# Conv2d 3x3 with 2x2 max pooling: merged row differences, one PSUM bank per image, 22 four-product steps and a new order of all operations

## The chip, the core and the metric

The kernel runs on one core of one Trainium2 chip. The metric is the device time in microseconds of one execution; lower is better. Names of engines in the profile: PE multiplies matrices (PEld loads their weights), DVE, ACT and POOL work element by element, SP issues most of the DMAs (queues of DMA issues are written SPq, ACTq, POOLq).

## The reference

Sixteen images with 64 channels of 64x64 are convolved with a 3x3 kernel (padding 1) to 128 channels, and the result is pooled by the maximum over 2x2.

```python
batch, c_in, h, w, c_out, k = 16, 64, 64, 64, 128, 3
x_pad = np.pad(x, ((0, 0), (0, 0), (pad, pad), (pad, pad)), mode='constant')
for kh in range(k):
    for kw in range(k):
        conv[b, co] += weight[co, ci, kh, kw] * x_pad[b, ci, kh:kh+h, kw:kw+w]
output[b, c, i, j] = np.max(conv[b, c, i*2:(i+1)*2, j*2:(j+1)*2])
```

## The kernel before

**The arithmetic.** Two conv rows that are pooled together, 2i and 2i+1, need four input rows: x(-1), x0, x1, x2. With g0, g1, g2 the three rows of the 3x3 weights, each of them three taps over columns, there are two ways to make them.

- A *five-product step* (K): the sum A = (g2-g1) x1 + g0 x(-1), the sum B = (g0-g1) x0 + g2 x2, and the common part R = g1 (x0 + x1). The pooled rows are max(A, B) + R. The products are called PA (two of them), PB (two) and PR. Only one row sum, KS = x0 + x1, has to be made.
- A *four-product step* (W): with E = x1 - x0, Z = x(-1) - x1, Y = x2 - x0 and S = x0 + x1, and GM = (g0+g2-g1)/2, GP = (g0+g1+g2)/2, the sum A is P2 = GM E plus P0 = g0 Z, the sum B is P2 with the other sign plus P3 = g2 Y, and P1 = GP S is common. Here four sums of rows (KS has one) are made on DVE or POOL, but PE has one product less.

Each product is three column taps (kw) for each of the two images of a pair. Channels are 64, so the two images of a pair lie on the two halves of the 128 rows of the array, and the two matmuls of a tap run at the same time, 512 columns each (8 output rows of 64).

**The steps.** A step is a quarter (8 pooled rows of 32) of a pair of images. There are 8 pairs x 4 quarters = 32 steps: 16 of K on the even pairs and 16 of W on the odd ones, one of each per turn of the loop. That makes 16 x 5 + 16 x 4 = 144 products of six matmuls, 864 matmuls.

**The way of a step.** PE writes A into one of four accumulators `acc` [128, 2, 8, 64], which hold two banks each, one for either image. For W, once P2 is there, ACT writes minus A into another accumulator as the start of B (`seed`, L301) while P0 is added to A. ACT copies A to SBUF (`evac`, L292, tile `ev`); DVE takes the maximum of B and `ev` in place (`rowmax`, L305); PE adds the common product PR or P1; ACT copies the odd columns (`odd`, L310, tile `od`); DVE takes the maximum of even columns and `od` (`colmax`, L324, tile `o`), and SP (in the end once ACT) stores it. All these work on 1024 elements per row (both images) or 512 after pooling of the rows; only in the last step on one image at a time. An accumulator is handed on through the list `free` when its last reader has been issued.

**Row operations.** `row_op` (L250) makes the sums of rows, 512 elements each: KS and WS on DVE, WZ and WY on POOL, WE on DVE up to step 4 and on POOL after that. `on_vector` and `on_gpsimd` tie each POOL operation behind the last one that DVE has done on SBUF. The W pairs lie in SBUF as fp32 in two buffers `wx`, the K pairs as bf16 in `kx`, cast by the DMA (POOL's queue, L95), except the first quarters, which come as fp32 and are cast by DVE (L340) and ACT (L347).

**Loads.** `wload(i + 4)` is issued behind the store of K's step i; `kload` brings half a pair of images at a time, one pair ahead, behind WY of quarters 1 and 2. So W quarters come four turns, K halves about three turns ahead.

**The order.** The scheduler is off; every engine works through its instructions in the order in which the program issues them. `HEAD`, `STEADY` (turns 4 to 12) and `TAIL` are lists written by hand. At the start the weights are loaded, combined (D2 = g2-g1, D0 = g0-g1, GM, GP), turned by PE (`turn`, L151) and copied out (`turn_out`, L163 to L169); eight matmuls on ones run ahead of that (L403).

Of the kernel before, what the change touches and what calls it, by code (L numbers as in the profile page):

```python
# [8 lines left out]


@with_exitstack
def kernel(
# [7 lines left out]

    nc = tc.nc
# [10 lines left out]
    NP = B // 2  # L45
    NQ = 4
    R = HO // NQ
    N = NP * NQ // 2
    assert N == 16
# [3 lines left out]
    row_pool = ctx.enter_context(tc.tile_pool(name="row_pool", bufs=2))  # L53
    ev_pool = ctx.enter_context(tc.tile_pool(name="ev_pool", bufs=3))
    od_pool = ctx.enter_context(tc.tile_pool(name="od_pool", bufs=3))
    o_pool = ctx.enter_context(tc.tile_pool(name="o_pool", bufs=4))
# [4 lines left out]
    acc = [psum.tile([128, 2, R, W], FP32, name=f"acc_{i}") for i in range(4)]  # L61
    free = deque(range(4))
    unset = set(range(4))

    SYNC = mybir.DependencyInfo(mybir.DependencyClass.Sync, mybir.DependencyReason.DATA)
    sbuf_op = [None]
# [5 lines left out]
    def on_vector(inst):  # L74
        sbuf_op[0] = inst
        return inst

    def on_gpsimd(inst):
        behind(inst, sbuf_op[0])
        return inst  # L80

# [4 lines left out]
    def chunk(q):  # L86
        return (2 * R * q + (q > 0), min(H, 2 * R * (q + 1) + 1))

    kx = {}
    wx = [const.tile([128, H + 2, W], FP32, name=f"wx_{i}") for i in range(2)]  # L90

    def kload(j, lo, hi):
        if j not in kx:
            kx[j] = kx_pool.tile([128, H, W], BF16, name="kx")
        return nc.gpsimd.dma_start(out=kx[j][:, lo:hi, :], in_=rows_of(2 * j, lo, hi))  # L95

    def wload(i):
        j, q = divmod(i, NQ)
        lo, hi = chunk(q)
        return nc.sync.dma_start(  # L100
            out=wx[j % 2][:, lo + 1 : hi + 1, :], in_=rows_of(2 * j + 1, lo, hi)
        )

    wraw = const.tile([CO, CI * K * K], FP32)
    nc.sync.dma_start(out=wraw, in_=weight.rearrange("a b c d -> a (b c d)"))  # L105
    _, khi = chunk(0)
    kfirst = const.tile([128, khi, W], FP32)
    nc.sync.dma_start(out=kfirst, in_=rows_of(0, 0, khi))
    klo2, khi2 = chunk(1)
    ksecond = const.tile([128, khi2 - klo2, W], FP32)  # L110
# [4 lines left out]
    for t in wx:  # L115
        nc.gpsimd.memset(t[:, 0, :], 0.0)
        nc.gpsimd.memset(t[:, H + 1, :], 0.0)

    D2, G0, D0, G2, GM, G1, GP = range(1, 29, 4)
    BLOCKS = {"D2": D2, "G0": G0, "D0": D0, "G2": G2, "GM": GM, "G1": G1, "GP": GP}
    wq = const.tile([CO, 29, CI], BF16)
    wt = const.tile([128, 28, CO], BF16)
    gsum = const.tile([CO, 3, CI], FP32)
# [5 lines left out]
    def slots(m):  # L131
        return wq[:, m : m + 3, :]

    def zero(t, h):
        return nc.tensor.matmul(
            acc[t][:, h], zeros[:, 0:128], zeros, start=True, stop=True, skip_group_check=True
        )

    turned = {}

    def turned_cols(m):
        lo, hi = BLOCKS[m] - 1, BLOCKS[m] + 3
        tp = acc[turned[m]][:, int(m == "G1")].rearrange("p a b -> p (a b)").bitcast(BF16)
        return lo, hi, tp[:, 0 : (hi - lo) * 128]

    def turn(m):
        turned[m] = turned["GM"] if m == "G1" else free.popleft()
        unset.add(turned[m])
        lo, hi, tp = turned_cols(m)
# [7 lines left out]
    def turn_out(m):  # L157
        if m != "GM":
            free.append(turned[m])
        lo, hi, src = turned_cols(m)  # L160
        dst = wt[:, lo:hi, :].rearrange("p a b -> p (a b)")
        if m == "GM":
            nc.scalar.mul(dst, src, 0.5)  # L163
        elif m == "GP":
            nc.vector.tensor_scalar_mul(out=dst, in0=src, scalar1=0.5)
        elif m in ("G0", "G2"):
            nc.scalar.copy(out=dst, in_=src)
        else:
            nc.vector.tensor_copy(out=dst, in_=src)  # L169


    def taps(t, m0, rows, start=False, skip=None, only=None):
        dst = acc[t]
        if start:
            unset.discard(t)
        for kw in (1, 0, 2):
            i0, i1 = 0, R
            if skip == 0:
                i0 = 1
            if skip == R - 1:  # L180
                i1 = R - 1
            o0, o1, c0, c1 = (0, W, 0, W) if kw == 1 else (1, W, 0, W - 1) if kw == 0 else (0, W - 1, 1, W)
            for half in range(2) if only is None else (only,):
                lo = half * CI
                nc.tensor.matmul(  # L185
                    dst[:, half, i0:i1, o0:o1],
                    wt[lo : lo + CI, m0 + kw - half, :],
                    rows(lo, i0, i1, c0, c1),
                    start=start and kw == 1,
                    stop=True,  # L190
                    skip_group_check=True,
                )

    def step1(t, q):
        first = q * R
        return lambda lo, i0, i1, c0, c1: t[lo : lo + CI, first + i0 : first + i1, c0:c1]

    def step2(t, first):
        return lambda lo, i0, i1, c0, c1: t[
            lo : lo + CI, first + 2 * i0 : first + 2 * (i1 - 1) + 1 : 2, c0:c1  # L200
        ]

    ta, tb = {}, {}

    def pa(i):
        j, q = divmod(i, NQ)
        t = ta["k", i] = free.popleft()
        taps(t, D2, step2(kx[j], 2 * q * R + 1), start=True)
        taps(t, G0, step2(kx[j], 2 * q * R - 1), skip=0 if q == 0 else None)

    def pb(i):
        j, q = divmod(i, NQ)
        t = tb["k", i] = free.popleft()
        taps(t, D0, step2(kx[j], 2 * q * R), start=True)
        taps(t, G2, step2(kx[j], 2 * q * R + 2), skip=R - 1 if q == NQ - 1 else None)

    def pr(i):
        taps(tb["k", i], G1, step1(row["ks", i // NQ], i % NQ))

    def p2(i):  # L220
        t = ta["w", i] = free.popleft()
        taps(t, GM, step1(row["we", i // NQ], i % NQ), start=True)

    def p0(i):
        taps(ta["w", i], G0, step1(row["wz", i // NQ], i % NQ))

    def p3(i):
        taps(tb["w", i], G2, step1(row["wy", i // NQ], i % NQ))

    def p1(i, h=None):  # L230
        taps(tb["w", i], GP, step1(row["ws", i // NQ], i % NQ), only=h)
# [4 lines left out]
    def row_out(name, i):  # L236
        j, q = divmod(i, NQ)
        if (name, j) not in row:
            row[name, j] = row_pool.tile([128, HO, W], BF16, name=name)
        return row[name, j][:, q * R : (q + 1) * R, :]  # L240
# [214 lines left out]
```

## Time and profile before

| | us |
|---|---|
| median of 3 runs (lowest, highest) | 108.33 (107.81, 108.77) |
| span of the profiled execution, first to last instruction | 106.18 |
| difference of median and span | 2.15 |
| first matmul of a product | 5.96 |
| last column maximum ends | 103.03 |

The profiled execution is one execution; its time is known by its span alone. The page shows each engine's busy time and share of the span; the "chain" goes back from the last instruction through what released each step. In a line of a group stand the source line, engine, operation, tiles, shapes and count, then the busy time and the mean in ns, then idle time ahead of them with what ended it. In a line of the timeline stand start and duration in us, engine, line, operation, tiles, shapes and the number of instructions merged. In a line of DMA issues the last two numbers are the size and the median time from issue to landing.

### The profile page before, as it was taken

The numbers are of one execution on the slowest core, as the hardware profiler recorded it, in microseconds if no ns is written. First come the engines' busy times: TensorE is split into PE (matmuls) and PEld (weight loads), VectorE is DVE, ScalarE is ACT, GpSimd is POOL, SyncE is SP. The second block draws the span as 40 slices with busy tenths as digits, with TensorE's granted clock in tenths as the row PEclk, the third lists the DMA queues.
The fourth block names the chain that finished last, engine by engine and source line by source line (L and its number), as shares of the span: only waits on it lengthen the run. The fifth ranks groups of instructions, "written<-read, shape, count | busy, mean of one in ns | idle before, by whom it ended". The sixth has DMA issues, their size and how long they took to land.

```text
span 106.2 us, 2337 instructions
## 1 busy us (share of the span) xinstructions
PE 98.7 (93%) x900; PEld 51.2 (48%) x900; DVE 82.3 (78%) x115; ACT 72.3 (68%) x92; POOL 60.6 (57%) x70
## 2 busy tenths in 40 slices
PE   7879999999999999999999999999999999999800
PEld 2444445555555555555555555555555555455300
DVE  1598989889797868696977868687879688668940
ACT  4628976776867677777677676767877776775620
POOL 6208691915439494949385694949293947653000
PEclk9999999999999999999999999999999999999975
DMA  2987999999968589999968399999966503232071
GB/s 53 370 269 269 228 152 314 264 304 304 316 245 211 190 177 187 219 298 195 337 253 208 124 210 202 265 257 213 385 188 167 195 4 122 78 107 96 0 247 49
DMA packets 12619, 21.96 MB, mean 207 GB/s; under 512 B 960, under 2 KB 9280, under 8 KB 12608
## 3 DMA queue, kind: packets, MB, share of 16 engines
q1 hardware_dynamic: 11312, 18.03, 52.9%
q0 software_dynamic: 1152, 3.65, 20.1%
q8 instruction: 7, 0.11, 0.4%
q10 hardware_dynamic: 144, 0.13, 0.4%
q14 instruction: 4, 0.03, 0.2%
HBM read 17.07 MB, written 8.39 MB: 240 GB/s over the span
## 4 chain that ended last, share of the span: by engine, by line
PE 84%; DVE 6%; DMA 4%; ACT 1%; issue 1%; SPq 0%; ACTq 0%; DVEq 0%
PE acc L185 83%; DVE acc L305 5%; DMA kfirst<-in_x_dram 4%; PE acc L151 1%; DVE o L324 1%; ACT od L310 1%; DVE kx L340 0%; SPq L105 0%; ACTq L333 0%; DVEq L305 0%
## 5 line engine op out<-in xcount | busy, mean ns | idle before, releaser
L185 PEld LDWEIGHTS <-wt 64*128 64x128 bf16 x864 | 48.6, 94 | 45.1 <-issue 1.8
L305 DVE TENSOR_TENSOR acc<-acc,ev 128x1024 f32<-128x1024 f32 (+1 forms) x34 | 39.5, 1166 | 11.9 <-PE acc L185 11.4
L185 PE MATMUL acc<-kx,wt 64*128 64x504 bf16 (+3 forms) x384 | 46.6, 373 | 0.6 <-DVE kx L340 0.6
L292 ACT COPY ev<-acc 128x1024 f32<-128x1024 f32 (+1 forms) x34 | 32.6, 964 | 12.5 <-PE acc L185 11.0
L250 POOL TENSOR_TENSOR wz<-wx 128x512 bf16<-128x512 f32 x16 | 20.3, 1271 | 30.3 <-DVE ws L250 24.3
L310 ACT COPY od<-acc 128x512 f32<-128x512 f32 (+1 forms) x33 | 19.0, 574 | 12.5 <-PE acc L185 11.5
L324 DVE TENSOR_TENSOR o<-acc,od 128x512 f32<-128x512 f32 (+1 forms) x33 | 22.1, 674 | 4.5 <-ACT od L310 4.4
L250 POOL TENSOR_TENSOR wy<-wx 128x512 bf16<-128x512 f32 x16 | 20.3, 1270 | 0.0
L301 ACT ACTIVATE acc<-acc 128x1024 f32<-128x1024 f32 x16 | 16.1, 1008 | 1.0 <-PE acc L185 0.5
L250 POOL TENSOR_TENSOR we<-wx 128x512 bf16<-128x512 f32 x11 | 14.1, 1278 | 0.1
L185 PE MATMUL acc<-ws,wt 64*128 64x504 bf16 (+1 forms) x96 | 13.3, 377 | 0.4 <-DVE acc L305 0.4
L185 PE MATMUL acc<-ks,wt 64*128 64x504 bf16 (+1 forms) x96 | 13.3, 377 | 0.1
L185 PE MATMUL acc<-we,wt 64*128 64x504 bf16 (+1 forms) x96 | 13.3, 377 | 0.0
L185 PE MATMUL acc<-wz,wt 64*128 64x504 bf16 (+1 forms) x96 | 13.2, 377 | 0.0
L185 PE MATMUL acc<-wy,wt 64*128 64x504 bf16 (+1 forms) x96 | 13.2, 377 | 0.0
L250 DVE TENSOR_TENSOR ws<-wx 128x512 bf16<-128x512 f32 x16 | 10.9, 684 | 0.0
L250 DVE TENSOR_TENSOR ks<-kx 128x512 bf16<-128x512 bf16 x16 | 6.7, 417 | 0.0
L95 POOL DMA_DIRECT2D kx<-in_x_dram x8 | 4.7, 589 | 2.6 <-DVE ks L250 2.6
L403 PE MATMUL acc<-const-bfloat16-1.0 128*128 128x512 bf16 x8 | 3.2, 572 | 0.8 <-PEq L436 0.8
L250 DVE TENSOR_TENSOR we<-wx 128x512 bf16<-128x512 f32 x5 | 3.6, 722 | 0.1
L354 DVE TENSOR_TENSOR wq<-wraw 128x192 bf16<-128x192 f32 x1 | 0.5, 500 | 2.6 <-DMA wraw<-in_weight_dram 2.6
L151 PE MATMUL acc<-ident,wq 128*128 128x128 bf16 x28 | 2.1, 220 | 0.4 <-DVE wq L354 0.4
(26 smaller groups left out, 15.9 us busy)
## 6 DMA issues: line engine op xcount, KB each, us to landing
out_dram<-o SPq DMA_DIRECT2D x31, 256.0 KB, 3.8
wx<-in_x_dram SPq DMA_DIRECT2D x8, 512.0 KB, 6.8
wx<-in_x_dram SPq DMA_DIRECT2D x4, 544.0 KB, 6.0
wx<-in_x_dram SPq DMA_DIRECT2D x4, 480.0 KB, 4.8
kx<-in_x_dram POOLq DMA_DIRECT2D x3, 528.0 KB, 8.3
kx<-in_x_dram POOLq DMA_DIRECT2D x3, 496.0 KB, 8.7
kfirst<-in_x_dram SPq DMA_DIRECT2D x1, 544.0 KB, 4.3
ksecond<-in_x_dram SPq DMA_DIRECT2D x1, 512.0 KB, 4.9
```

The costliest lines, as they stand in the source:

```text
L95: return nc.gpsimd.dma_start(out=kx[j][:, lo:hi, :], in_=rows_of(2 * j, lo, hi))
L151: nc.tensor.transpose(tp[:, (j - lo) * 128 : (j - lo + 1) * 128], wq[:, j : j + 2, :].rearrange("a b c -> a (b c)"), ident,)
L185: nc.tensor.matmul(dst[:, half, i0:i1, o0:o1], wt[lo : lo + CI, m0 + kw - half, :], rows(lo, i0, i1, c0, c1), start=start and kw == 1, sto ...
L250: return engine.tensor_tensor(out=row_out(name, i), in0=row_in(t, f + a, pad), in1=row_in(t, f + b, pad), op=op)
L292: nc.scalar.copy(out=ev[g][:, halves(h)], in_=acc[ta[g]][:, halves(h)])
L301: nc.scalar.mul(acc[t], acc[ta["w", i]], -1.0)
L305: nc.vector.tensor_tensor(out=t, in0=t, in1=ev[g][:, halves(h)], op=MAX)
L310: nc.scalar.copy(out=od[g][:, halves(h)], in_=acc[tb[g]][:, halves(h), :, 1::2])
L324: nc.vector.tensor_tensor(out=o, in0=acc[tb[g]][:, s, :, 0::2], in1=od[g][:, s], op=MAX)
L354: on_vector(nc.vector.tensor_sub(out=slots(D2), in0=g2, in1=g1))
L403: warm = nc.tensor.matmul(acc[n // 2][:, n % 2], ones[:, 0:128], ones, start=True, stop=True, skip_group_check=True)
```

## The change

Almost every line of the kernel is written anew; the arithmetic of a step stays. What differs:

1. **10 K steps and 22 W steps** instead of 16 and 16. `SEQ` gives their sequence. K has pairs 0 and 1 and half of pair 2, W the rest. That is 10 x 5 + 22 x 4 = 138 products.
2. **One difference over 16 rows, V** (`rv`), takes the place of Z and Y: input rows shifted by two, subtracted for all 16 rows at once, 1024 elements. Its even rows are minus Z, its odd rows Y; P0 and P3 read every second row of it. E changes its sign too, so A has the other sign, `evac` of W multiplies by -1 and `seed` copies as it is.
3. **One bank for each image.** `acc` is eight tiles of one bank. `EV`, `SE`, `MX`, `OD`, `CM` exist for each image by itself: 64 each (44 of SE), of 512 elements, or 256 after pooling of the rows. Products are issued for each image too; two that stand next to each other in the order, on different images, are interleaved tap by tap, and they may be different products. Four products have no partner. The first K step's products are halved (4 rows each) to begin on half of the load.
4. **Loads** of a quarter at a time for both kinds: 24 quarters as fp32 on SP (step 0's in two pieces, K step 3 cast by ACT), 8 casting loads on POOL's queue. From step 7 on, the load of step s waits for both column maxima of step s-7 (`paced`, `AHEAD`). There are four `wx` buffers; the row sums have a pool of 8 small tiles, V one of 6, `ev` and `od` 8, `o` 12.
5. **Engines and order.** `ORDER`, one list of tokens, gives the order of all instructions, the engine of each row operation (v, a, g for DVE, ACT, POOL) and the bank of each sum. DVE has 10 KS, 14 E, 8 S and 9 V, POOL 8 E, 14 S and 13 V. A POOL row operation is still tied behind the last one of DVE in the list (`row_op`).

```diff
+SEQ = "KWWKWWKWWKWWKWWWKWWKWWKWWKWWKWWW"
+ORDER = """
+LW c.g0:a c.GS:v c.D0:v c.GM:v T.G0:0 c.g2:a LX.1 c.g1:a T.D0:1 LX.0a T.GM:2 c.D2:v E.1:v TV.G0:a
...
+CM.6.0 PBa.9.0:5 P0.7.1 OD.6.1 EV.7.1 MX.9.1 MX.8.0 LK.12 P2.7.0:2 P3.7.1 ST.3 CM.6.1 PBb.9.0
+P2.8.1:6 MX.7.1 S.10:g SE.7.0:1 S.7:g SE.8.1:0 E.10:v P1.8.0 PR.9.1 MX.9.0 OD.9.1 CM.9.1 OD.8.0
+S.11:g P1.7.1 P0.7.0 OD.7.1 EV.7.0 E.11:g P3.7.0 P0.8.1 CM.7.1 MX.7.0 PR.9.0 P3.8.1 PAa.12.1:4
...
+ST.23 S.30:g ST.26 EV.30.0 OD.29.0 MX.30.1 EV.31.1 P1.31.0 P3.31.1 MX.30.0 P1.30.1 P1.30.0 CM.29.0
+OD.31.0 MX.31.1 CM.31.0 OD.30.1 ST.25 CM.30.1 ST.29 ST.31.0 P1.31.1 OD.30.0 CM.30.0 OD.31.1 ST.30.1
+ST.30.0 CM.31.1 ST.31.1
+"""
...
-    acc = [psum.tile([128, 2, R, W], FP32, name=f"acc_{i}") for i in range(4)]
-    free = deque(range(4))
+    acc = [psum.tile([128, R, W], FP32, name=f"acc_{i}") for i in range(8)]
...
+    last_row = [None]
+    def row_op(e, out, in0, in1, op):
+        inst = eng[e].tensor_tensor(out=out, in0=in0, in1=in1, op=op)
+        if e == "g":
+            behind(inst, last_row[0])
+        else:
+            last_row[0] = inst
...
+    AHEAD = 7
+    def paced(s, inst):
+        for l in (0, 1):
+            behind(inst, done.get((s - AHEAD, l)))
...
+    def load_cast(s):
+        p, lo, hi = chunk(s)
+        paced(s, nc.gpsimd.dma_start(out=kx_of(p)[:, lo:hi, :], in_=rows_of(p, lo, hi)))
...
-    def wz(i):
-        on_gpsimd(row_op(nc.gpsimd, "wz", i, -1, 1, SUB))
-    def wy(i):
-        on_gpsimd(row_op(nc.gpsimd, "wy", i, 2, 0, SUB))
...
+    def rv(s, e):
+        p, q = place[s]
+        t = row["V", s] = v_pool.tile([128, 2 * R, W], BF16, name="wv")
+        f = 2 * R * q
+        u = wx[p % NWX]
+        row_op(e, t, u[:, f + 2 : f + 2 + 2 * R, :], u[:, f : f + 2 * R, :], SUB)
...
+        "P0": ("A", pw("G0", "V", False, 2, 0)),
+        "P3": ("B", pw("G2", "V", False, 2, 1)),
...
+    def evac(s, l):
+        t = ev[s, l] = ev_pool.tile([128, R, W], FP32, name="ev")
+        if SEQ[s] == "W":
+            nc.scalar.mul(t, acc[bank["A", s, l]], -1.0)
+        else:
+            nc.scalar.copy(out=t, in_=acc[bank["A", s, l]])
...
+    def flush():
+        for group in zip(*unit):
+            for tap in group:
+                tap()
+        unit.clear()
```

In a token such as `P0.7.1` stand the product (or operation), the step and the image; `SE.7.0:1` writes bank 1, `S.10:g` runs on POOL, `LX` loads as fp32, `LK` loads and casts, `ST` stores.

More of the change, by code (lines that the diff above doesn't have):

```diff
@@ L1 @@
-from collections import deque
 from contextlib import ExitStack
@@ L89 @@
-    kx = {}
[L90 to L102, printed above, removed]
@@ L104, with chunk @@
-    wraw = const.tile([CO, CI * K * K], FP32)
[L105 to L110, printed above, removed]
+    def chunk(s):
+        p, q = place[s]
+        same = any(place[t] == (p, q - 1) and SEQ[t] == SEQ[s] for t in range(N))
+        lo = 2 * R * q + 1 if same else max(0, 2 * R * q - 1)
+        return p, lo, min(H, 2 * R * (q + 1) + 1)
@@ L175, in taps @@
+    def taps(name, s, l, part):
+        side, of = PRODUCTS[name]
+        block, i0, i1, rows, first = of(s, l, part)
+        t = bank[side, s, l]
+        if first:
             unset.discard(t)
         for kw in (1, 0, 2):
[L177 to L181, printed above, removed]
-            o0, o1, c0, c1 = (0, W, 0, W) if kw == 1 else (1, W, 0, W - 1) if kw == 0 else (0, W - 1, 1, W)
[L183 to L192, printed above, removed]
@@ L211, in pb @@
[L211 to L225, printed above, removed]
@@ L406 @@
-        if n == 3:
-            behind(wload(0), warm)
-    kx[0] = kx_pool.tile([128, H, W], BF16, name="kx")
-    def run(order):
-        for s in order.split():
-            name, *args = s.split(".")
-            steps[name](*map(int, args))
-    run(HEAD)
-    for i in range(FIRST, LAST + 1):
-        for s in STEADY.split():
-            steps[s[:-2]](i + int(s[-2:]))
-    run(TAIL)
+        nc.tensor.matmul(
+            acc[n], ones[:, 0:128], ones, start=True, stop=True, skip_group_check=True
+        )
```

457 lines of the change are left out of this document (253 added, 204 removed).

## The prediction

> **What bounds the kernel now.** I read the page first (busy shares, chain by engine), then the chain of waits in order of time, the groups by form, and the timeline at both ends. From the page and the chain in order of time:
>
> ```profile
> PE 98.7 (93%) x900; PEld 51.2 (48%) x900; DVE 82.3 (78%) x115; ACT 72.3 (68%) x92; POOL 60.6 (57%) x70
> PE 84%; DVE 6%; DMA 4%; ACT 1%; issue 1%; SPq 0%; ACTq 0%; DVEq 0%
> ...
> 5.96 1.39 PE acc L185 x12
> ...
> 9.64 81.42 PE acc L185 x756
> ...
> 102.61 0.42 DVE o L324
> ```
>
> PE sets the time: 756 matmuls follow one another in 81.42 us, 0.1077 us each (two run at once, one on each half of the rows). 864 x 0.1077 = 93.05 us. With 0.9 us of transposes after the first product, PE could go from 5.96 to 99.9; its last six matmuls end at 100.9, so it loses about 1.0 us in all. Behind it come two pairs of odd-column copy and column maximum (to 103.03) and the last store (3.15 us, to 106.18). The profiled span is 106.18 and the median of the runs 108.33, so I add 2.15 us to a span.
>
> The prices come from groups by form (mean ns) and from the distance between neighbours on the timeline of DVE and ACT:
>
> ```profile
> L305 DVE TENSOR_TENSOR acc<-acc,ev 128x1024 f32<-128x1024 f32 x30 | 36.8, 1228 | 11.7 <-PE acc L185 11.4 <-ACT ev L292 0.2
> L305 DVE TENSOR_TENSOR acc<-acc,ev 128x512 f32<-128x512 f32 x4 | 2.7, 696 | 0.2
> L324 DVE TENSOR_TENSOR o<-acc,od 128x256 f32<-128x256 f32 x2 | 0.8, 424 | 1.0 <-ACT od L310 0.8
> L250 POOL TENSOR_TENSOR wy<-wx 128x512 bf16<-128x512 f32 x16 | 20.3, 1270 | 0.0
> L357 POOL TENSOR_TENSOR gsum<-wraw 128x192 f32<-128x192 f32 x1 | 0.8, 824 | 2.4 <-DVE wq L356 2.4
> ```
> ```profile
> 44.79 1.23 DVE L305 TENSOR_TENSOR acc<-acc,ev 128x1024 f32<-128x1024 f32 x1 [0.85 <-PE acc L185]
> 46.00 0.69 DVE L324 TENSOR_TENSOR o<-acc,od 128x512 f32<-128x512 f32 x1
> 46.60 0.42 DVE L250 TENSOR_TENSOR ks<-kx 128x512 bf16<-128x512 bf16 x1
> 46.94 0.69 DVE L250 TENSOR_TENSOR ws<-wx 128x512 bf16<-128x512 f32 x1
> ```
>
> Back to back, DVE starts the next instruction about 0.08 us before the last one ends: 0.60 us for 512 elements, 0.34 for one of 0.42 us, 1.21 for 1024 from acc. By that rule the 696 ns row costs 0.61 and the 424 ns row 0.34.
>
> **The change, part by part.**
>
> *Matmuls.* 10 five-product and 22 four-product steps make 138 products of six, 828 full matmuls (24 extra come from halving early products, two halves for one): 828 x 0.1077 = 89.2 us, 3.9 less.
>
> *Order of the two row halves.* Before, they alternate throughout. Now four products stand alone in the queue (three matmuls on one half) and in some 66 places the order flips. Strictly in order, each single would leave the other half idle (six pair times of 0.215, 1.3 us) and each flip cost the 20 ns between two partners (1.3 us). The last products before show it: they are issued as three on one half and then three on the other, yet take what six alternating ones take.
>
> ```profile
> 98.20 0.83 PE L185 MATMUL acc<-ws,wt 64*128 64x512 bf16 x6
> ...
> 100.07 0.83 PE L185 MATMUL acc<-ws,wt 64*128 64x512 bf16 x6 [0.39 <-DVE acc L305]
> ```
>
> So I cost the order at 0, between 0 and 2.6. The Trainium skill ("TensorE: Matmul & The Clock Gate", Part 3) says that matmuls start and end strictly in program order; by that rule the sum would be 2.6 us longer, and the row above disagrees.
>
> *Start and end of PE.* The first product now needs a four-product chunk of 1152 columns instead of 1088 as second load of the queue. The old one landed at 5.46; 33 KB more at its rate (557 KB from 3.68 to 5.46) is 0.1, and its difference on DVE 0.7: start at 6.3. Eight transposes (0.6) and one zeroing matmul (0.2) follow it. PE's end is 6.3 + 0.8 + 89.2 = 96.3. Behind it one copy (0.38), one maximum (0.43) and the store (3.15), no longer two of each in turn, since each image has its own bank: 100.3. That is the span if PE never waits.
>
> *DVE.* 64 row maxima x 0.61 = 39.0; 64 column maxima x 0.34 = 21.8; nine merged differences of 1024 elements, 1.14 each by the 1024 row = 10.3; 14 E x 0.60 = 8.4; 8 S x 0.60 = 4.8; 10 KS x 0.34 = 3.4; weights, turn-outs and casts of the head 3.4. Sum 91.1, where before gives 80.4 in the same way: halving the instructions doubles their fixed part. From 3.7 (weights landed) DVE could end at 94.8; with the store 97.95. It may lose 2.35 us before it, not PE, sets the end. This is the tightest new number.
>
> *ACT.* 108 copies of 512 at 0.48 (two followed each other by that at 94.61), 64 of 256 at 0.27, 6 us of head: 75. 20 us are free; hidden, if not late.
>
> *POOL.* 22 operations of 512 at 1.23 are 27.1. A merged difference of 1024 isn't in the trace: at least 1.23, at most 2 x 1.23; the 192 and 512 rows give 1.4 ns per element, so 1.95. 13 of them 25.4, casting loads 4.7: 57. Before, the two separate differences cost 2.46 together. Hidden.
>
> *DVE against POOL.* One DVE row operation began before under a running POOL operation:
>
> ```profile
> 10.38 1.26 POOL L250 TENSOR_TENSOR wy<-wx 128x512 bf16<-128x512 f32 x1
> ...
> 11.31 0.88 DVE L250 TENSOR_TENSOR we<-wx 128x512 bf16<-128x512 f32 x1
> ```
>
> It took 0.88 instead of 0.69: 0.20 longer, when 0.33 of the POOL operation was left. Maxima over acc don't suffer (1.23 under POOL and without). The kept order ties each POOL operation behind DVE's last row operation, but not DVE's next behind POOL. Before, KS and WS come together once a step and POOL is done by then. Now 41 row operations are spread among 35 of POOL. I set both on a clock of 0.323 us per product and image along the written order: 15 of the 41 meet a running POOL operation, with 12.3 us left of these in sum; less 0.13 each, 10.3. The written order isn't time, and some stand just behind POOL's end, so the bounds are 0 and 10.3; I take the middle, 5.2. The Trainium skill ("SBUF — State Buffer", Who interferes with whom) says that a VectorE instruction with two SBUF inputs and a GpSimd instruction reading SBUF exclude one another for a whole instruction; the 0.88 row agrees, and by that rule the price goes to the upper end.
>
> *Loads.* A load of step s now waits for the column maxima of step s-7, and the stores ahead of it on SP wait too; a casting load also stands behind POOL's differences. On the same clock, step 12's is issued at about 30.4 (behind V.8) and wanted by PE at 35.0: 4.6 us. Steps 25, 28, 22, 9 have 5.5, 6.1, 6.5, 6.7. From the issues:
>
> ```profile
> kx<-in_x_dram POOLq DMA_DIRECT2D x1, 256.0 KB, 7.5
> kx<-in_x_dram POOLq DMA_DIRECT2D x1, 240.0 KB, 7.9
> ```
>
> Same size, but in the busiest stretch (DMA 0.90 from 10 to 40 us, 0.64 from 70 to 90). Fp32 loads of some 512 KB took 4.3 us (kfirst) to 6.8 (the usual wx), so an estimate for a quiet casting load is 7.5 x 4.3/6.8 = 4.7. At 4.7 the lack is 0.1, at 7.5 it is 2.9 + 2.0 + 1.4 + 1.0 + 0.8 = 8.1; at 6.0, which I take, 1.9. Two thirds of that lies under DVE's lateness, which postpones PE's want: 0.7.
>
> *Sum.* 97.95 + 0.4 (DVE waiting for loads in the head) + 5.2 + 0.7 = 104.25; with 2.15, **106.4**, 1.8% less.
>
> **Rivals.**
> 1. *Nothing is late* (neither port nor loads beyond 0.7): PE bounds, 100.3 + 0.7 + 2.15 = 103.2. For it: PE lost only 1.0 before. Against: DVE would need 97% of its time.
> 2. *DVE bounds, slower.* All 15 meetings cost in full: 97.95 + 0.4 + 10.3 + 0.4 = 109.05, 111.2. Place: KS, E and S on DVE behind V on POOL (V.8, V.18, V.26, V.29). It decides from 8 us of stops. For it: the 0.88 row; against: the order often puts DVE's operation right behind POOL's end.
> 3. *Casting loads late.* 7.5 us each: 100.3 + 8.1 = 108.4, 110.6. For it: every such load before took 7.5 or more; against: half the size of most, and spread out.
> 4. *Strict program order on PE*: 106.4 + 2.6 = 109.0, no change. Against: the six matmuls above.
>
> **How the numbers follow.** 1% (about what a measurement of this kernel can tell) is 107.25 to 109.4. Rival 1 and what lies near it 0.19; my forecast (104.7 to 107.25) 0.36; within 1%: forecast with more port time 0.12, rival 4 0.06; rival 2 0.17; rival 3 0.10. Faster 0.55, same 0.18, slower 0.27. The range is from rival 1 to rival 2, 103.2 to 111.2; the likeliest case alone 104.7 to 107.25.
>
> **What would show it.** PE: 889 instructions, products still 0.1077 each where dense, singles without a gap. DVE busy near 90 us and over 85% of the span. Row operations on DVE (we, ws, wv, ks) longer than 0.69, 0.69, 1.22, 0.42 where POOL runs: their excess is the port's price. PE's idle time put down to kx loads at steps 12 and 25 tells rival 3; to DVE's maxima, rival 2. A merged difference on POOL near 2.0 us. After the last matmul 4.0 us to the end. Wrong would be: DVE with much idle time while PE waits, or ACT as releaser.

## The result, and the profile after

The changed kernel takes 112.69 us (median of 4 runs, 112.57 to 112.99), the kernel before 108.53 on the same chip: ratio 1.040, 95% interval 1.036 to 1.044. It is 4% slower. The forecast was 106.4, 1.8% faster, and its range ended at 111.2. The profiled execution took 112.76 us with a span of 110.99, so 1.77 us lie outside the span. Of some kernels below, single executions lie over 1.5% above the fastest one (137.11 against 132.14 us in 4); the ranges include them, the ratios leave them out.

First the page of the changed kernel: busy time and share of the span by engine, then the chain by engine.

```profile
PE 100.8 (91%) x889; PEld 53.6 (48%) x889; DVE 95.5 (86%) x179; ACT 85.4 (77%) x185; POOL 64.6 (58%) x65
...
PE 26%; DVE 14%; DMA 12%; POOL 7%; ACT 6%; issue 3%; SPq 1%; DVEq 0%; ACTq 0%
```

Before, PE made up 84% of the chain and DMA 4%. Now PE has 26% and DMA 12%, and the rest hops between the engines. No engine is the bound; something hands its lateness round. The chain in order of time (start, duration, what) shows what:

```profile
44.88 5.64 DMA wx<-in_x_dram
...
79.53 7.88 DMA kx<-in_x_dram
...
87.46 12.12 PE acc L340 x108
...
106.08 0.82 PE acc L340 x3
...
106.92 0.38 ACT od L374
...
107.32 0.42 DVE o L379
```

The end is reached through two loads: an fp32 load of SP issued at 44.88 us and a casting load issued at 79.53 that took 7.88 us. TensorE's last matmuls end at 106.90 (96.3 in the forecast, if TensorE never waits), and behind them come one copy, one maximum and the store, 4.1 us (forecast 4.0).

Why the loads are late stands in the waits (who waited for whom: us in total, times, longest). The first line is of SP's queue, where L245 issues the fp32 loads:

```profile
SPq L245 <- DVE o L379: 63.4, 15, 16.1
```
```profile
DVE we L181 <- DMA wx<-in_x_dram: 4.8, 6, 1.9
...
POOL we L181 <- DMA wx<-in_x_dram: 2.9, 1, 2.9
...
PE acc L340 <- DMA kx<-in_x_dram: 1.8, 2, 0.9
```

SP stood 63 us before loads, every time for a column maximum (L379): that is the pacing. In turn DVE, POOL and TensorE waited for the data. The largest single stop, at 29 us on the timeline:

```profile
28.16 1.24 PE L340 MATMUL acc<-kx,wt 64*128 64x504 bf16 x8
28.35 0.69 DVE L181 TENSOR_TENSOR we<-wx 128x512 bf16<-128x512 f32 x1 [1.93 <-DMA wx<-in_x_dram]
...
30.09 0.42 DVE L379 TENSOR_TENSOR o<-acc,od 128x256 f32<-128x256 f32 x1
30.25 2.36 POOL L181 TENSOR_TENSOR wv<-wx 128x1024 bf16<-128x1024 f32 x1 [1.77 <-DVE wv L181]
30.43 0.69 DVE L370 TENSOR_TENSOR acc<-acc,ev 128x512 f32<-128x512 f32 x1
30.56 0.37 PE L340 MATMUL acc<-we,wt 64*128 64x512 bf16 x1 [1.17 <-DVE o L379]
```

The load of step 8 was issued at 21.34 us and landed at 28.25. Its own maxima, those of step 1, had ended at 19.34; but on SP it stands behind the load of step 7, which waited for the maxima of step 0 until 20.94, so the pacing of one load holds the next one too. E.8 and V.7 stand in DVE's order ahead of the column maximum CM.5.0 (the line at 30.09), which frees the bank that the next product of step 8 writes. So E.8's wait held DVE for 1.93 us, POOL stood idle for 1.77 us before V.8, and TensorE stopped 1.33 us longer than a pair of matmuls takes. The bracket at PE names the maximum; the cause stands two instructions ahead of it on DVE.

A simple measure serves for all kernels below: TensorE's *lateness* is how far its products lag behind one full matmul every 0.1077 us, counted from the start of its first product. (At a span of 110.99: first product at 6.35 + 89.2 of matmuls + lateness + 4.11 behind the last.) It is 11.3 us here at the end of the last matmul; in the kernel before it was 1.9. Of the 11.3, the head (to 10.5 us) has 2.5 us; E.8 1.3; E.15, whose load is the one at 44.88, 0.5; the casting loads of steps 25 and 28 1.08 and 1.09; two stops for row operations of POOL at 60 and 62 us 0.22 and 0.38; the last products 0.9; the rest is many small pieces.

The rows that answer to the prediction's prices (mean ns):

```profile
L370 DVE TENSOR_TENSOR acc<-acc,ev 128x512 f32<-128x512 f32 x64 | 42.8, 691 | 2.1 <-ACT ev L355 1.4 <-PE acc L340 0.3 <-ACT ev L357 0.2
...
L181 DVE TENSOR_TENSOR wv<-wx 128x1024 bf16<-128x1024 f32 x9 | 11.6, 1299 | 0.0
...
L181 DVE TENSOR_TENSOR ws<-wx 128x512 bf16<-128x512 f32 x8 | 6.3, 788 | 0.0
L181 DVE TENSOR_TENSOR ks<-kx 128x512 bf16<-128x512 bf16 x10 | 5.2, 517 | 0.0
```
```profile
L181 POOL TENSOR_TENSOR wv<-wx 128x1024 bf16<-128x1024 f32 x13 | 30.7, 2358 | 12.4 <-DVE we L181 4.5
```

Row maxima cost what they should. KS is 517 instead of 417 ns and S 788 instead of 684: these met POOL. A merged difference on POOL costs 2.36 us, not 1.95.

### The profile page after: what moved, and what is told of

It is laid out like the page before. It is cut to its first block, busy times and chain, and to the rows that moved or that the text cites. A ratio compares the mean times of both kernels' runs of the same rounds, so it can differ in the third digit from the quotient of the medians.

```text
span 111.0 us, 2491 instructions
## 1 busy us (share of the span) xinstructions
PE 100.8 (91%) x889; PEld 53.6 (48%) x889; DVE 95.5 (86%) x179; ACT 85.4 (77%) x185; POOL 64.6 (58%) x65
## 3 DMA queue, kind: packets, MB, share of 16 engines
q1 hardware_dynamic: 12480, 21.34, 60.3%
## 4 chain that ended last, share of the span: by engine, by line
PE 26%; DVE 14%; DMA 12%; POOL 7%; ACT 6%; issue 3%; SPq 1%; DVEq 0%; ACTq 0%
PE acc L340 26%; DMA kx<-in_x_dram 7%; DMA wx<-in_x_dram 5%; DVE acc L370 5%; DVE wv L181 4%; DVE o L379 4%; ACT ev L355 4%; POOL ws L181 3%; POOL wv L181 2%; ACT od L374 1%; ACT acc L366 1%; POOL we L181 1%; DVE we L181 1%; SPq L388 1%; DVE ws L181 1%
## 5 line engine op out<-in xcount | busy, mean ns | idle before, releaser
L340 PE MATMUL acc<-wv,wt 64*128 64x504 bf16 (+1 forms) x264 | 55.4, 377 | 0.3 <-POOL wv L181 0.2
L340 PE MATMUL acc<-kx,wt 64*128 64x504 bf16 (+5 forms) x264 | 48.6, 355 | 2.9 <-DMA kx<-in_x_dram 1.8
L370 DVE TENSOR_TENSOR acc<-acc,ev 128x512 f32<-128x512 f32 x64 | 42.8, 691 | 2.1 <-ACT ev L355 1.4
L181 POOL TENSOR_TENSOR wv<-wx 128x1024 bf16<-128x1024 f32 x13 | 30.7, 2358 | 12.4 <-DVE we L181 4.5
L340 PE MATMUL acc<-we,wt 64*128 64x512 bf16 (+1 forms) x132 | 32.3, 377 | 1.7 <-DVE o L379 1.2
L340 PE MATMUL acc<-ws,wt 64*128 64x512 bf16 (+1 forms) x132 | 33.4, 377 | 0.2
L355 ACT ACTIVATE ev<-acc 128x512 f32<-128x512 f32 x44 | 26.1, 602 | 5.2 <-PE acc L340 4.6
L366 ACT COPY acc<-acc 128x512 f32<-128x512 f32 x44 | 25.4, 579 | 5.1 <-DVE o L379 2.8
L374 ACT COPY od<-acc 128x256 f32<-128x256 f32 x64 | 23.1, 377 | 5.5 <-PE acc L340 5.0
L379 DVE TENSOR_TENSOR o<-acc,od 128x256 f32<-128x256 f32 x64 | 24.9, 415 | 1.6 <-ACT od L374 1.3
```

What stands on the lines that cost most here:

```text
L181: inst = eng[e].tensor_tensor(out=out, in0=in0, in1=in1, op=op)
L340: yield lambda kw=kw, o0=o0, o1=o1, c0=c0, c1=c1: nc.tensor.matmul(acc[t][:, i0:i1, o0:o1], wt[l * CI : l * CI + CI, BLOCKS[block] + kw - ...
L355: nc.scalar.mul(t, acc[bank["A", s, l]], -1.0)
L366: nc.scalar.copy(out=acc[b], in_=acc[bank["A", s, l]])
L370: nc.vector.tensor_tensor(out=t, in0=t, in1=ev[s, l], op=MAX)
L374: nc.scalar.copy(out=t, in_=acc[bank["B", s, l]][:, :, 1::2])
```

## The experiments

Three theories. **L, late loads:** the pacing, and places behind other instructions on SP's and POOL's queues, make loads late, and waiting engines pass it on. **P, port:** row operations of DVE stop while POOL works, and the merged difference makes POOL's stretches longer. **D, DVE full:** the halved instructions fill DVE, and loads only show it. Each kernel was timed beside the kernel before.

### 1. The pacing taken away

```diff
-    AHEAD = 7
+    AHEAD = 99
```

> The changed kernel without the tie of a load to the column maxima of seven steps before; the order stays, so on SP a load still stands behind the stores written ahead of it. Theory L (late loads cost most: 1.33 + 0.48 + 1.08 + 1.09 us of PE gaps after the head are ended by a load or by a difference that waited for one): the gaps at E.8 and the casting loads shrink, 1.5 to 4 us faster, 108.7 to 111.2. Theory P (the port that DVE and POOL share, and POOL's 2.36 us for a merged difference, set the pace): loads are only what comes last, within 1 us of 112.7. Theory D (DVE, with 91 us of work in doubled instructions, is full): within 1 us of 112.7 as well.

Measured: 111.05 us (110.53 to 111.36), ratio 1.025 (1.021 to 1.028). The stop at E.8 is gone, the lateness falls from 11.3 to 8.3 us. Two stops stay, 1.42 us for the casting load of step 25 and 0.79 for that of step 28: they stand behind differences on POOL and were issued at 70.29 and 77.05, landing 7.4 and 7.8 us later. L holds for 1.6 us, and shows that the pacing is only part of it.

### 2. All loads from step 7 on earlier, with a pacing of twelve steps

```diff
-    AHEAD = 7
+    AHEAD = 12
```

In `ORDER` each load of a step s from 7 on stands directly behind both CM of step s-12 (if there is none, behind the first loads); among themselves they keep their order.

> The changed kernel with every load from step 7 on moved ahead in the order, behind the column maxima of twelve steps before instead of seven, on both queues. Theory L: no load is late after the head, the four gaps (4.0 us) go and what stood behind them: 107.5 to 109. Theory P: 111.5 to 113, and the excess of DVE's row operations under POOL stays near 2.7 us. Theory D: 111 to 113, DVE's idle time turns into other idle time.

Measured: 113.83 us (113.35 to 115.13), ratio 1.049 (1.045 to 1.054): slower than the changed kernel, the opposite of what L expected. The timeline tells why:

```profile
55.91 0.57 POOL L254 DMA_DIRECT2D kx<-in_x_dram  x1 [2.69 <-DVE o L379]
56.50 2.35 POOL L181 TENSOR_TENSOR wv<-wx 128x1024 bf16<-128x1024 f32 x1
56.90 4.26 DVE L181 TENSOR_TENSOR wv<-wx 128x1024 bf16<-128x1024 f32 x1
58.80 1.26 POOL L181 TENSOR_TENSOR we<-wx 128x512 bf16<-128x512 f32 x1
```

A casting load sits on POOL's queue and waits there for a column maximum, so POOL stood for 2.69 us; V.15 behind it came late and met V.17 of DVE, which took 4.26 us instead of 1.22, through two operations of POOL. TensorE stopped 2.0 us for V.15, and at 31 us 2.4 us for V.8, late in the same way. The experiment had moved a wait onto a busy engine; it does not speak against L, and it shows what P can do.

### 3. POOL's merged differences left out

```diff
+        if e == "g":
+            behind(nc.gpsimd.memset(t, 0.0), last_row[0])
+            return
         row_op(e, t, u[:, f + 2 : f + 2 + 2 * R, :], u[:, f : f + 2 * R, :], SUB)
```

> The changed kernel with the 13 merged differences of POOL replaced by a fill with zeros of the same tile (their products come out as zero): it reads nothing and is shorter. Theory P: DVE's row operations lose most of their excess of 2.7 us, POOL some 15 to 25 us of work, and the time falls by 2.5 to 5 us, 107.7 to 110.2. Theory L: the casting loads stand earlier on POOL's queue, but the loads stay tied to the column maxima: less than 2 us, 110.7 to 112.7. Theory D: less than 1 us.

Measured: 111.53 us (110.87 to 112.49), ratio 1.030 (1.024 to 1.036). The excess of DVE's row operations falls from 2.6 to 0.1 us, the time by 1.2. The stops for the loads stay (1.32 us at E.8, 0.51 and 0.56 for steps 25 and 28). (Those for the casting loads are shorter than the 1.08 and 1.09 us of the changed kernel; this profile is of an execution of 112.49 us, the slowest of four.) So P is real and the smaller part.

### 4. POOL's row operations no longer tied behind DVE's

```diff
-        if e == "g":
-            behind(inst, last_row[0])
-        else:
-            last_row[0] = inst
+        return inst
```

> The changed kernel without the ties of POOL's row operations behind DVE's last one. The profile shows POOL waiting for DVE's row operations, 11.4 us once at the start and about 13 us after that. Theory P: POOL and DVE meet more often, DVE's row operations grow by more than the 2.7 us of excess they have, 112.5 to 115. Theory L: POOL starts earlier, the casting loads behind it too, and the time falls by 0.5 to 2 us, 110.7 to 112.2. Theory D: it grows with DVE's excess, like P.

Measured: 132.74 us (132.14 to 137.11), ratio 1.223 (1.219 to 1.228). DVE's row operations lost 24.4 us to 16 meetings. One of them on the timeline:

```profile
21.67 0.57 POOL L251 DMA_DIRECT2D kx<-in_x_dram  x1 [5.05 <-DVE o L376]
...
21.94 4.45 DVE L181 TENSOR_TENSOR ws<-wx 128x512 bf16<-128x512 f32 x1
22.27 2.36 POOL L181 TENSOR_TENSOR wv<-wx 128x1024 bf16<-128x1024 f32 x1
24.57 1.26 POOL L181 TENSOR_TENSOR ws<-wx 128x512 bf16<-128x512 f32 x1
26.32 0.41 DVE L181 TENSOR_TENSOR ks<-kx 128x512 bf16<-128x512 bf16 x1
```

S.5 of 0.69 us took 4.45: it began while POOL was issuing a casting load (first line) and stood until both operations of POOL behind that were through. The tie is what keeps P small in the changed kernel.

### 5. Three loads moved up their queues, without pacing

```diff
-    AHEAD = 7
+    AHEAD = 99
 S.13:g
+LX.15
 ST.8
 ST.0
 E.13:g
...
-LX.15
...
 V.20:g
+LK.25
...
-LK.25
 E.23:g
...
 E.24:g
+LK.28
...
-LK.28
```

> The changed kernel without the wait of its loads on the column maxima of seven steps before, and with three loads further up their queues: the casting loads of steps 25 and 28 (behind V.20 and behind E.24 on POOL), the load of step 15 ahead of the stores of steps 8 and 0 on SP. Nothing else. Late loads (L): without the pacing alone TensorE still stopped 1.42 and 0.79 us for the casting loads of steps 25 and 28 and 0.29 us behind the load of step 15; these go, 111.05 - 2.5 = 108.6 us, between 108.0 and 109.2. DVE full (D): the loads only showed what DVE lacks; the stops are named after DVE then, 110.4 to 111.2. Port (P): moved casting loads push differences of POOL under row operations of DVE, 111 to 113.

Measured: 108.03 us (107.33 to 108.39), ratio 0.998 (0.995 to 1.002). L's number, and inside its bounds; D and P had expected 110 and more. Three places in a list are worth 3.0 us beyond the pacing's 1.6; together that is 4.7 us (4.5 by the ratios), and the change had lost 4.2. Its chain is TensorE's again:

```profile
1.65 6.29 DMA kf<-in_x_dram
...
10.72 68.23 PE acc L340 x629
...
81.29 2.37 POOL wv L181
...
83.70 10.69 PE acc L340 x95
```

629 matmuls in 68.23 us, 0.1085 each. Of the 6.0 us of lateness left, 2.5 are collected before 11 us. (In the same lines: a late merged difference of POOL at 81.29.)

### 6. The same three moves with the pacing kept

```diff
-    AHEAD = 99
+    AHEAD = 7
```

(against 5)

> The changed kernel with its pacing kept, and only the three loads of e7_lead moved up (the casting loads of steps 25 and 28 on POOL, the load of step 15 on SP). This tells the place in the queue from the wait. Place alone: the stops for steps 25 and 28 (1.08 and 1.09 us) and at E.15 (0.48) go, the one at E.8 (1.33) stays: 112.7 - 2.3 = 110.4 us. Wait: the casting loads now wait on POOL's queue for column maxima of seven steps before, POOL stands still behind them, its row operations come later and meet DVE's: 111.5 to 114.

Measured: 112.58, 113.23, 115.85 and 116.03 us, median 114.54; the spread is too wide for an interval of the ratio, and the profiled execution is that of 113.23. That places alone would do (110.4) is refuted. TensorE no longer stops for steps 25 and 28, but still 1.73 us at E.8, and now 1.18 at E.27, whose fp32 load was issued at 78.02 and landed at 85.20, just in front of where the stop for step 28 had been. Not by the mechanism that I had named, which could not come: `paced` ties a load to maxima that stand ahead of it in the list, and the loads of steps 25 and 28 now stand ahead of the maxima of steps 18 and 21, so these two carry no wait at all (step 25's was issued at 67.48 us, the maxima of step 18 ended at 69.01 and 70.92). POOL stood only 1.4 us for the other casting loads (1.2 in the changed kernel). What the run shows is the pacing of the loads that were not moved: the next paced load takes the place of the one cured (step 27's was issued right behind the last maximum of step 20, which ended at 77.96). Why single runs reach 116 stays open.

### 7. The head in another order

Against 5, in the tokens of SP and PE (banks 0 and 5, 2 and 6 are exchanged throughout, and the turn-outs and casts follow):

```diff
-LX.1
 LX.0a
 LX.0b
+LX.1
...
-P2.1.1:5 P2.1.0:6
-PAa.0.1a:0 PAa.0.0a:2
+PAa.0.1a:5 PAa.0.0a:6
 PAa.0.0b PAa.0.1b
+P2.1.1:0 P2.1.0:2
```

> As e7_lead, and the head in another order: the two parts of step 0 are loaded ahead of step 1, and TensorE does the first products of step 0 (PAa), then P2 of step 1, then PAb; two pairs of banks are exchanged for that. The stop of 1.24 to 1.31 us behind the first product of step 1 goes, and P0 of step 1 starts 1.0 to 1.7 us earlier. L: 1.0 to 1.5 us below e7_lead, 107.0 to 107.8. D: DVE starts its row maxima no earlier than before and sets the end, within 0.5 us of e7_lead.

Measured: 110.09 us (109.33 to 111.94), ratio 1.015 (1.006 to 1.025), 2.1 us slower than 5. The load of step 1, now third, landed at 9.42 instead of 5.60 us, and P2.1 stopped TensorE for 2.97 us (in the profiled execution, the slowest of the four with 111.94 us). Being first in the queue is worth more than I had taken; that the loads behind it, already issued, slow it too, is what 8 tries.

### 8. Loads of the head held back

Against 5:

```diff
-            eng[e].tensor_tensor(out=slots("D2"), in0=g2, in1=g1, op=SUB)
+            mark[5] = eng[e].tensor_tensor(out=slots("D2"), in0=g2, in1=g1, op=SUB)
...
-            eng[e].tensor_tensor(out=slots("D0"), in0=g0, in1=g1, op=SUB)
+            mark[2] = eng[e].tensor_tensor(out=slots("D0"), in0=g0, in1=g1, op=SUB)
...
     def paced(s, inst):
+        behind(inst, mark.get(s))
```

> As e7_lead, with the loads of steps 2 and 5 held on SP behind two weight operations of DVE (c.D0, c.D2), so that they are issued at about 4.6 and 5.4 us instead of 2.6 and 3.1; all else the same. In e7_lead 2.6 of the 5.8 us that TensorE loses lie before 11.5 us, 1.31 of them behind the first product, where it waits for the cast of step 0, whose load landed at 7.94, 2.3 us behind the one ahead of it. If the loads queued behind it share the engines with it, it lands 0.6 to 1.2 us earlier and that stop shrinks by as much. L (PE loses by loads alone): 0.6 to 1.2 us below e7_lead, ratio to before about 0.987 to 0.993. D (in e7_lead DVE idles only 3.1 us after 10 us, so DVE sets the end and a gain of PE alone is lost again): same as e7_lead within 0.3 us, 0.995 to 1.002.

Measured: 107.44 us (107.16 to 108.23), ratio 0.993 (0.991 to 0.996): 0.7% faster than the kernel before. The first load of step 0 lands at 6.40 instead of 7.94 us, and TensorE goes on without the stop of 1.3 us:

```profile
6.52 0.82 PE L342 MATMUL acc<-we,wt 64*128 64x512 bf16 x6 [0.18 <-ACT wt L227]
7.22 0.50 PE L342 MATMUL acc<-kx,wt 64*128 64x256 bf16 x6
...
15.85 0.37 PE L342 MATMUL acc<-kx,wt 64*128 64x512 bf16 x1 [0.51 <-ACT kx L174]
```

The last line is the price: the load of step 3, last of that queue, now lands at 15.16 us (13.66 in 5), and TensorE stops 0.67 us for it. So 0.6 of 1.3 us remain.

### 9. Two moves on DVE, then two attempts at the load of step 3

9a, against 8:

```diff
+XE.0a:v XE.0b:v
 E.2:v
...
-XE.0a:v
-XE.0b:v
...
-KS.28:v
...
 MX.28.0
+KS.28:v
 S.29:v
```

9b, against 9a:

```diff
+LX.3
 LX.4
...
-LX.3
```

9c, against 8, with KS.28 moved as in 9a:

```diff
 E.5:v
+LX.7
...
-        behind(inst, mark.get(s))
+        behind(inst, last_row[0] if s == 7 else mark.get(s))
```

> As e12_hold, and two moves in the order of DVE alone: the even casts of step 0 stand ahead of E.2, where DVE idled 1.03 us for the load of step 2, and KS.28 stands behind MX.28.0 instead of ahead of MX.27.1, where it ran 1.33 us instead of 0.42 under S.26 of POOL. DVE gets back 0.5 and 0.9 us. D: 0.7 to 1.4 us below e12_hold, 106.5 to 107.4 us, faster than the kernel before by about 1%. L: no gain over e12_hold, since no load is moved. P (meetings of DVE and POOL count in full where DVE is full): the part of KS.28, 0.9 us.

> As e9_fast, with the load of step 3 ahead of the load of step 4 on SP. Holding the loads of steps 2 and 5 took TensorE's stop behind its first product from 1.31 to 0.08 us, but the load of step 3, last in that queue, then landed at 14.85 instead of 13.66 and TensorE stopped 0.56 us for it at 14.8. L: that stop goes, 0.5 us below e9_fast, ratio to before 0.989 to 0.993. D: DVE, whose row operation E.5 waits there for nothing that moves, keeps the end, 0.995 to 0.999.

> As e12_hold, with the loads of steps 7 and 8 held on SP until E.5 of DVE is done (they are issued at about 14 instead of 6.8 and 7.5 us, and wanted at 24 and 33 us), and KS.28 moved behind MX.28.0 as in e9_fast. In e12_hold the load of step 3 landed at 15.16 us, 1.26 us behind the start of step 7's landing, and TensorE stopped 0.67 us for it. L: step 3 lands 0.4 to 1.0 us earlier, the stop goes, 0.4 to 0.7 us below e12_hold, ratio to before 0.986 to 0.991. If the loads ahead of it, not behind it, are what it waits for: no difference, 0.992 to 0.997.

Measured: 9a 107.82 us (ratio 0.9965, 0.994 to 0.999), 9b 108.98 (1.006, 1.004 to 1.009), 9c 108.68 (0.999, 0.995 to 1.003). None beats 8. In 9a DVE loses 1.1 us to meetings instead of 2.0, and TensorE ends no earlier (101.54 us against 101.53): D's expectation fails. In 9b step 3 lands at 13.07 us and its stop is gone, but step 4 lands at 14.56, E.5 needs its last row and holds KS.0 behind it on DVE, and TensorE stops 0.60 us there. In 9c step 3 lands at 13.84 and that stop is gone too, but the loads held now stand in the way of the next ones (step 9 lands at 25.28 us, 22.76 in 8), and the lateness grows by 1.3 us between 26 and 36 us. In all three each gain for one load was a loss for another.

### 10. The column maximum left out

```diff
-        t = od[s, l] = od_pool.tile([128, R, WO], FP32, name="od")
-        nc.scalar.copy(out=t, in_=acc[bank["B", s, l]][:, :, 1::2])
+        nc.scalar.copy(out=ot[s][:, l], in_=acc[bank["B", s, l]][:, :, 1::2])
```

> As e13_step3, with the column maximum left out: ACT's copy of the odd columns writes the output tile, and DVE has 64 instructions (21.8 us) less to do. DVE is then far from full; products, loads, POOL and ACT are the same, and the tail is shorter by one column maximum of 0.43 us. L (nothing but loads, with DVE's fullness of no account): TensorE's end moves by less than 0.5 us, 0.4 to 1.0 us below e13_step3. D (DVE's fullness is the second thing that keeps the gain away): TensorE's stops after 15 us (some 2.5 us in e9_fast) go as well, 2.5 to 3.5 us below e13_step3, 103.5 to 105.0 us.

Measured: 108.17 us (107.32 to 108.41), ratio 0.998 (0.995 to 1.001), 0.8 below 9b. The page:

```profile
PE 99.5 (94%) x889; PEld 54.9 (52%) x889; DVE 79.9 (75%) x115; ACT 85.1 (80%) x185; POOL 64.2 (60%) x65
```

DVE has 14 us less to do and waits 10 us for TensorE, and yet TensorE's last matmul ends at 102.54 us (9b: 102.36). The 0.8 us are the shorter tail (3.7 instead of 4.5 us). DVE's amount of work does not set the end. The run does not leave everything else alone, though: DVE, ahead of its old pace, meets POOL more often, and the excess of its row operations rises from 1.2 us (9b) to 7.7 (KS.19 took 1.91 instead of 0.42 us under V.18). What a less full DVE would be worth with the meetings unchanged, it does not show. D falls as the bound, here and in 9a.

### 11. POOL's merged differences left out, with the loads in time

The edit of 3 on the kernel of 8.

> As e12_hold, with POOL's 13 merged differences replaced by fills with zeros, so that their products are zero; products, loads and DVE's work stay. It shows what POOL costs once the loads come in time. DVE's meetings with V (S.20, E.27, E.31: 0.73 us) and TensorE's stops for a late V (0.35 us at 83 us, 0.22 at 96) go if P is the rest: 0.6 to 1.3 us below e12_hold. L: no difference beyond 0.3 us.

Measured: 106.18 us (106.01 to 106.75), ratio 0.981 (0.978 to 0.985), 1.26 below 8. The chain:

```profile
9.45 83.72 PE acc L345 x770
```

770 matmuls without a break that counts, 0.1087 each. In the two profiled executions the lateness that comes up from 25 us on is 3.1 us in 8 and 2.2 here; before that, step 3's load landed earlier here (14.15 against 15.16 us). So POOL's merged differences cost 0.9 (from the lateness) to 1.3 us (from the medians) once the loads are in time: P is the second cause, about the size that it had in 3. The fill takes POOL less time as well, so the port and a late POOL are not told apart here.

### 12. Merged differences on POOL taken apart again

```diff
+        for z in (slice(0, None, 2), slice(1, None, 2)) if e == "g" else (slice(None),):
+            hi, lo = u[:, f + 2 : f + 2 + 2 * R, :], u[:, f : f + 2 * R, :]
+            row_op(e, t[:, z], hi[:, z], lo[:, z], SUB)
```

> As e7_lead, but each of the 13 merged differences on POOL is made as two of 512 elements (even and odd rows of the same tile), as the kernel before makes them; the 9 on DVE stay merged. If merging is what it was meant to be on POOL, a saving, this is slower; by the rows it is not: 2 x 1.27 = 2.54 against 2.36 us, 13 x 0.18 = 2.3 us more on POOL, which has 40 us free. P: DVE can slip in between the two, so a meeting lasts at most 1.27 us instead of 2.36: 0 to 0.5 us faster. L and D: within 0.5 us of e7_lead, 107.6 to 108.5.

Measured: 108.63 us (108.05 to 110.87), ratio 1.002 (0.998 to 1.006); 5, on which it is based, has 0.998. No gain from the gap between the two: the pair takes 2.54 us instead of 2.36, and the excess of DVE's row operations rises from 2.0 to 3.6 us.

### 13. Single parts of the change in the kernel before

```diff
 # 13a: wz and wy on POOL as one merged difference, the signs moved as in the change
 # 13b: evac, seed, rowmax, odd, colmax as two instructions, one for each image
```

> The kernel before, with one part of the change alone: its two POOL differences wz and wy of 16 steps become one merged difference of 1024 elements (the signs move into the copies that ACT makes anyway). P: a merged difference measured 2.36 us against 2 x 1.27, so POOL has 2.9 us less to do and nothing waits for it; 108.0 to 108.9, no difference. If one unbroken stretch of 2.36 us meets row operations of DVE that two of 1.27 let through, 109 to 111. L and D: 108.0 to 108.9.

> The kernel before, with another part of the change alone: every copy of sums, seed, row maximum, odd column copy and column maximum is split into two, one per image, as the changed kernel has them; products, loads, POOL and order stay. D: doubled instructions cost DVE 31 x (2 x 0.34 - 0.60) = 2.5 us and nothing for the row maxima (2 x 0.60 against 1.21), ACT some 30 x 0.1 + 33 x 0.05 = 5 us; DVE then has 83 of 97 us, ACT 77; if that shows on the path already, 109.5 to 111. L and P: hidden behind TensorE, 107.8 to 109.0 (the end itself may be shorter, since one image's maximum starts earlier).

Measured: 13a 108.15 us, ratio 1.001 (0.997 to 1.006): merging alone does nothing. 13b 109.55 us, ratio 1.0125 (1.006 to 1.019): halving the instructions costs 1.4 us even where TensorE is the bound. Its lateness grows from 1.9 to 3.5 us, 0.7 of that before 17 us (a stop of 0.40 us at 14.4 for a load's cast, 0.11 for a difference of POOL), and the first product starts 0.2 us later. I had expected it hidden or 109.5 to 111; it is the lower edge of the second.

## Why the prediction was wrong, step by step

- **Loads: the step that failed.** It priced lateness at 0.7 us; 4.7 us go with the pacing and three places in queues (5), another 0.6 with the hold in the head (8). Three things were wrong. (a) Only casting loads were looked at; the fp32 loads of SP were given 0.4 us in the head and nothing behind it, although the text itself says that they wait for step s-7. E.8 (1.33 us) and E.15 (0.48) are those. I had counted a load's lead from its issue to TensorE's want, and the want comes sooner: a row operation on DVE stands before it, and DVE works in order, so what is behind it waits too. (b) The landing was taken as 6.0 us; the casting loads that stopped TensorE took 7.1 and 7.9 us, with leads of 6.0 and 6.8 (forecast 5.5 and 6.1). Rival 3, casting loads at 7.5 us, is right for these two steps; step 12, which it put first, landed in 5.4 and stopped nothing. (c) Two thirds were written off as "under DVE's lateness". By 9a and 10 DVE's work does not set the end, so there was nothing to hide under.
- **The path.** The sum ran along DVE (91.1 us of work, 97.95 with the store), called "the tightest new number". DVE's work was close: in 5 DVE ends at 102.6, less 3.65 at the start, 4.4 idle and 2.0 of meetings it is 92.6 us. But 0.9 us given back to DVE (9a) and even 14 us taken out of it (10, with more meetings) leave TensorE's end where it was: DVE is nearly full and not the bound. The sum should have run along TensorE: 6.3 + 89.2 + lateness + 4.0.
- **Matmuls, 89.2 us.** Right: 0.1085 to 0.1087 each over long stretches, small stops included.
- **Order of the row halves at 0, bounds 0 to 2.6.** Right for the flips: in the changed kernel six matmuls take 0.648 us in the median with a flip behind them (58 pairs of products) and without one (66). Products without a partner are not free: of three of them the three matmuls took 0.65, 0.65 and 0.41 us in the changed kernel and 0.43, 0.51 and 0.36 in that of 8, where half of a pair's six takes 0.32; why the two kernels differ stays open. The rule of the Trainium skill ("TensorE: Matmul & The Clock Gate", Part 3) of a strict program order would have cost the upper bound, rival 4; two of these products cost what it says (0.33 us each), the flips and the last products before do not show it.
- **First product at 6.3 us.** 6.35. But behind it TensorE stopped 1.24 us for step 0's load, which lands 1.5 us sooner when two loads issued after it are held back (8). The forecast had only the transposes and the zeroing there (0.8); the head's lateness is 2.5.
- **V on POOL at 1.95 us.** 2.36, near the upper bound of 2.46, so merging saves 0.18 us, not 0.5. "Hidden" was wrong as well: 0.9 to 1.3 us (11).
- **Port at 5.2 us, bounds 0 to 10.3.** The mechanism is right, the size too high for DVE's side: 2.6 us in seven meetings. Rival 2, all 15 of them in full, did not come. The Trainium skill ("SBUF — State Buffer", Who interferes with whom) has the kind right, and the trace agrees: KS.19 of DVE, two SBUF inputs, took 1.15 instead of 0.42 us under V.18, and row maxima, one input in PSUM, stayed at 0.69. It doesn't follow for a kernel that ties the two engines that every meeting counts in full.
- **Outside the span:** 1.77 instead of 2.15 us. The 2.15 set the median of the runs against the span of another execution; where an execution of the kernel before has both its time and its span on record, 1.7 to 1.8 us lie between them. Nothing changed there; the forecast was 0.4 too high in this term.

In sum: loads cost 5.3 us (112.69 to 107.44; 5.0 by the ratios), POOL's merged differences another 1.3 (to 106.18, in a kernel that leaves them out). That this is near the forecast's 106.4 is chance: its 5.2 us of port stood in DVE's sum, which does not set the end, and so covered lateness of TensorE that it had no term for (4.0 us are left in 11, 1.3 of them before 11 us). Left open: where the small pieces of that come from, and what part of the loads' landing time (4.2 to 7.9 us for casting loads of one kernel) is the stores' doing; no run moved the stores alone.

## What to carry to other kernels

When a change makes TensorE's work shorter, ask of every load, not only the slowest kind, when it is issued, what it waits for on its queue, and which in-order engine stands still if it is late. A wait that paces transfers is cheap only on a queue that does nothing else, and only if the lead covers the worst landing; put on POOL's queue it delays that engine's arithmetic, which then collides with DVE's. Cure lateness at its source and look at what is late next: here three entries moved up a list brought 3 us once the pacing was gone and nothing while it stayed (5 and 6), while later attempts in the crowded head only handed the stop on.

## What the hardware showed that was not expected

- A row operation of DVE that waits for POOL can be passed over a second time: S.5 (lines in 4) stood through V.4 and through the operation behind it, 4.45 us instead of 0.69, and in 2 V.17 stood through two operations in the same way (4.26 instead of 1.22). V.4's record starts 0.33 us behind S.5's, but POOL was already busy with the issue of a casting load. Where POOL was idle when DVE's operation began, DVE kept its place and POOL's operation grew, 1.70 instead of 1.27 us here (kernel of 4):

```profile
9.80 0.69 DVE L181 TENSOR_TENSOR we<-wx 128x512 bf16<-128x512 f32 x1 [0.68 <-DMA wx<-in_x_dram]
...
9.93 1.70 POOL L181 TENSOR_TENSOR ws<-wx 128x512 bf16<-128x512 f32 x1 [7.27 <-DMA wx<-in_x_dram]
```

  The Trainium skill ("SBUF — State Buffer", Who interferes with whom) says of VectorE's two-port modes that whoever issues first keeps the ports for the whole instruction; these lines show the same for two SBUF inputs. Whether the issue of the load is what put POOL ahead of S.5 is not shown: an issue with no operation of POOL right behind it cost DVE nothing (KS.12 of the changed kernel, begun at 40.54 us during one, took 0.41 us).
- When a load lands depends on what is issued behind it as well as ahead: the 576 KB load of step 1 landed at 5.60 us as the first and at 9.42 us as the third, behind 544 KB (7); with two loads behind it held back, step 0's came 1.5 us sooner (6.40 against 7.94 us, 8).
- On POOL 1024 elements in one instruction take 2.36 us and 512 take 1.27: by these two the fixed part is only 0.18 us (an estimate), and merging saves no more than that.
